# Weight low parts on VectorE alone, keys split straight into their own half, and a planner that may wait before it chooses

## The chip, the cores and the metric

The kernel runs on one core of a Trainium2 chip. The metric is device time in microseconds (us) of one execution. A core has five instruction streams that matter here: TensorE (PE in the profile, with its weight loads as PEld), VectorE (DVE), ScalarE (ACT), GpSimd (POOL) and SyncE (SP), which issues all of this kernel's DMAs.

## The reference

One layer of a hybrid decoder, 512 tokens of width 1024, all in float32. Cut to what matters:

```python
proj = rmsnorm(x, ln_mix_g) @ w_in                # 1024 -> 7728 columns
dq, dk = rope(rmsnorm(...)), rope(rmsnorm(...))   # 8 heads x 2 x 64
y_diff = (softmax(q0 k0) - lam * softmax(q1 k1)) @ v     # causal, 8 heads
k_cmp, v_cmp = gelu(blocks(k) @ w1) @ w2 ...      # compressed keys and values
y_nsa  = g0 * cmp + g1 * selected + g2 * window   # 16 heads, 4 key groups
mixed  = sig(m0) * (y_diff @ w_proj_diff) + sig(m1) * (y_nsa @ w_proj_nsa)
x = x + mixed @ w_out
x = x + square(relu(rmsnorm(x) @ w_mlp_up)) @ w_mlp_down
```

## The kernel before

**Two parts for a number.** A float32 operand of a matmul is held as a high part (a copy rounded to the type `F32R`) and a low part (operand minus high part), and a product is three matmuls: high by high, high by low, low by high. `split(hi, lo, src)` makes the parts: a copy that ACT or DVE does, then a subtraction on the engines in `lo_engs`.

**Weights.** `WStream` brings the weights as pieces of 128 x 1024 (`wraw`, two buffers) by a DMA of SP, and splits each in two halves of 512 columns into `whi` and `wlo` (two buffers each). `add`, in the last part of the kernel, hands every piece but those of the first chunk to the stream with `("DVE", "POOL")` as the engines that may subtract. The first chunk's four pieces are handed over near the start, also with both.

**The streams.** The PE order is first written by generators that a small driver (`Pe.run`) interleaves: a filler (all the large matmuls in a fixed plan: projections, merge gates, output projection, MLP) and four hot streams (rope, compressed keys, values, scores). The projections and the attention share the time up to about 660 us; after that only the output projection and the MLP are left.

**Keys.** `rope_stream` takes a finished projection chunk, normalises and rotates it (`norm_rope`, on ACT, DVE and POOL, with the power for the inverse square root on POOL), transposes a pair of key vectors into one PSUM bank (`ptp`, two banks) and calls `k_dups`. The two vectors of a pair lie in partitions 0 to 63 and 64 to 127. The scores need each vector in all 128 partitions (the query's high part meets it in one half, the low part in the other). `k_dups` splits the bank into one SBUF buffer `kp` (a single buffer), and four DMAs copy from there to the upper and the lower half of two key tiles `kk` (three buffers). There are 12 such pairs: 8 for the differential heads, 4 for the other branch.

**The planner.** `note` collects every instruction; `flush` then orders them by a list schedule with a price for each instruction (`price`), a latency between engines, and one shared resource, `port`: an instruction for which `ported` is true (a POOL instruction, or a DVE instruction of four kinds with all operands in SBUF, if its largest operand has 64 elements or more) isn't planned to run beside another such one. An instruction with more than one allowed engine goes to the one that takes it first. All instructions are then emitted from line 357, so every group of the profile has that line, and names of tiles tell them apart. The plan sets the order on each engine; on the chip each engine runs its list in order and waits for semaphores.

The lines that choose when the port is taken:

```python
if not put_off[-1][1].port[e]:
    p, op = put_off.pop()
else:
    p, op = put_off.pop(0)
...
op.start = max(t, self.port) if op.port[e] else t
```

Of the kernel before, what the change touches and what calls it, by code (L numbers as in the profile page):

```python
# [12 lines left out]
F32R = mybir.dt.float32r  # L13
AF = mybir.ActivationFunctionType
OP = mybir.AluOpType
# [116 lines left out]
class Sched:  # L132
# [34 lines left out]
    def price(self, eng, method, aps, k):  # L167
        if "accum_out" in k:
            aps = [x for x in aps if x is not k["accum_out"]]
        n = max(self.size(x) for x in aps)  # L170
        psum = any(self.tiles[x.tensor.name].space == "PSUM" for x in aps if x.tensor.name in self.tiles)
        if eng == "PE":
            if method == "transpose":
                return 113.0
            return max(113.0, 5.5 + self.size(aps[-1]) * 0.4315)
        if eng == "ACT":
            return (51 if psum else 93) + n * 0.8333 + (93 if "accum_out" in k else 0) + (
                93 if any(self.size(x) == 1 for x in aps[1:]) and n > 1 else 0)
        if eng == "DVE":
            ptr = sum(1 for x in aps[1:] if self.size(x) == 1) if n > 1 else 0  # L180
            if method in ("tensor_scalar", "tensor_copy") and not psum:
                return 69 + n * 0.52 + 61 * ptr
            if method == "memset":
                return 8 + n * 1.04
            if method == "reciprocal":
                return 69 + n * 6.25
            return 69 + n * 1.042 + 61 * ptr
        if eng == "POOL":
            if k.get("op") == OP.pow:
                return 300 + n * 165.0  # L190
            return 150 + n * 2.1
        return 20.0
# [2 lines left out]

    def ported(self, eng, method, aps, k):

        if max(self.size(x) for x in aps) < 64:
            return False
        if eng == "POOL":  # L200
            return k.get("op") != OP.pow
        return eng == "DVE" and method in self.TWICE and not any(
            self.tiles[x.tensor.name].space == "PSUM" for x in aps if x.tensor.name in self.tiles)

# [67 lines left out]
    def flush(self):  # L272

        ops, self.ops = self.ops, []
        self.wait = {e: [] for e in self.free}
        ok = {e: [] for e in self.free}
        fresh, again = [], set()
        for op in ops:
            for b in op.bufs:
                if b.group is None or b in again:  # L280
                    continue
                again.add(b)
                if b.granted:
                    self.held[b.group] += 1
                else:
                    fresh.append(b)
        for b in fresh:
            self.held.setdefault(b.group, 0)
            self.queue.setdefault(b.group, []).append(b)
        for op in ops:  # L290
            op.left, op.ready = 1, 0.0
            for d in op.deps:
                if d.left == -1:
                    op.ready = max(op.ready, d.end + self.lat(d.eng, op.eng, op.deps[d]))
                else:
                    d.users.append(op)
                    op.left += 1
            for b in op.bufs:
                if not b.granted:
                    b.waiting.append(op)  # L300
                    op.left += 1
        for g in list(self.queue):
            self.grant(g, 0.0)
        for op in ops:
            self.arm(op)
        done = []
        while len(done) < len(ops):
            best = None
            for e in self.free:
                for h, k in ((self.wait[e], 2), (ok[e], 1)):  # L310
                    while h and h[0][k].left == -1:
                        heapq.heappop(h)
                t = self.free[e] if ok[e] else max(self.free[e], self.wait[e][0][0]) if self.wait[e] else None
                if t is not None and (best is None or t < best[0]):
                    best = (t, e)
            assert best is not None, "no instruction can go on"
            t, e = best
            while self.wait[e] and self.wait[e][0][0] <= t:
                _, p, op = heapq.heappop(self.wait[e])
                if op.left == 0:  # L320
                    heapq.heappush(ok[e], (p, op))
            p, op = heapq.heappop(ok[e])
            if op.port[e] and self.port > t:
                put_off = [(p, op)]
                while ok[e] and put_off[-1][1].port[e]:
                    z = heapq.heappop(ok[e])
                    if z[1].left == 0:
                        put_off.append(z)
                if not put_off[-1][1].port[e]:
                    p, op = put_off.pop()  # L330
                else:
                    p, op = put_off.pop(0)
                for z in put_off:
                    heapq.heappush(ok[e], z)
            op.eng = e
            op.start = max(t, self.port) if op.port[e] else t
            op.end = op.start + op.ways[e][1]
            if op.port[e]:
                self.port = op.end
            self.free[e] = op.end  # L340
            if op.dma:
                self.hw = max(op.end, self.hw) + op.dma[0]
                self.dma = max(self.hw + 650, self.dma) + op.dma[1]
                op.end = self.dma
            op.left = -1
            done.append(op)
            for u in op.users:
                u.ready = max(u.ready, op.end + self.lat(e, u.eng, u.deps[op]))
                self.arm(u)
            for b in op.bufs:  # L350
                b.left -= 1
                b.end = max(b.end, op.end)
                if b.left == 0 and b.group is not None:
                    self.held[b.group] -= 1
                    self.grant(b.group, b.end + 150)
        for op in sorted(done, key=lambda o: o.start):
            op.ways[op.eng][0](*op.a, **op.k)  # L357
            op.ways = op.a = op.k = op.users = op.deps = None
# [68 lines left out]
def hybrid_block(ctx: ExitStack, tc: tile.TileContext, x, ln_mix_g, w_in, dqg, dkg, lq1, lk1, lq2, lk2,  # L427
# [4 lines left out]
    V, A, P, T, Q = (Engine(sched, n, e) for n, e in (("DVE", nc.vector), ("ACT", nc.scalar), ("POOL", nc.gpsimd),  # L432
                                                      ("PE", nc.tensor), ("SP", nc.sync)))
# [3 lines left out]
    def pool(stack, name, space="SBUF"):  # L437
        kw = {} if space == "SBUF" else {"space": getattr(MT, space)}
        return Pool(sched, stack.enter_context(tc.tile_pool(name=name, bufs=1, **kw)), space)
# [10 lines left out]
    def f(ap):  # L450
        return ap.bitcast(F32)
# [4 lines left out]
    def copy(out, src, engs=("ACT", "DVE")):  # L456
        sched.note([(e, COPY[e], getattr(sched.engs[e], COPY[e])) for e in engs], (out, src), {})

    def tt(out, a, b, op, engs=("DVE",)):
        sched.note([(e, "tensor_tensor", sched.engs[e].tensor_tensor) for e in engs], (out, a, b), {"op": op})  # L460

    def split(hi, lo, src, hi_engs=("ACT", "DVE"), lo_engs=("DVE",)):

        copy(hi, src, hi_engs)
        tt(lo, src, f(hi), OP.subtract, lo_engs)
# [11 lines left out]
    ws = WStream(wp, split)  # L477
# [87 lines left out]
    with ExitStack() as ps:  # L565
        pg = pool(ps, "pg", "PSUM")
        pscore = pool(ps, "pscore", "PSUM")
        ptr = pool(ps, "ptr", "PSUM")
        pav = pool(ps, "pav", "PSUM")

        att = pool(ps, "att")
# [316 lines left out]

        def k_dups(pt, key):

            kp = att.tile([128, 2, 512], F32R, tag="kp", bufs=1, name="kp")
            split(kp[:, 0, :], kp[:, 1, :], pt)
            if key[0] == "dk":
                kk = k_tile()
                dst = [kk[:, s] for s in range(2)]
            else:

                if key[2] == 0:
                    for s in range(2):
                        group_keys[key[1], s] = k_tile()  # L900
                dst = [group_keys[key[1], s][:, key[2]] for s in range(2)]
            for s in range(2):
                for d in range(2):
                    Q.dma_start(f(dst[s][d * 64:(d + 1) * 64]), f(kp[s * 64:(s + 1) * 64]))
            return dst

        jobs = []
# [633 lines left out]
        def add(gen, pieces):  # L1541
            for piece in pieces:
                load, width = piece if isinstance(piece, tuple) else (piece, 1024)
                ws.add(load, ("DVE", "POOL"), width)
            plan.append(gen)

        def eight(src):
# [101 lines left out]
```

## Time and profile before

| | before |
|---|---|
| time, median of 3 runs | 1096.38 us (1095.64 to 1096.85) |
| profiled execution | 1096.69 us, of which its span 1094.9 us |
| PE busy | 1053.8 us, 96% of the span |
| DVE busy | 766.2 us, 70% |
| POOL busy | 477.0 us, 44% |
| ACT busy | 465.6 us, 43% |
| mean granted TensorE clock | 0.990 |

The span is from the first to the last instruction of the profiled execution. Busy time counts instructions from start to end, including time in which one is held up inside; it isn't a rate. A row of a timeline gives the start, the duration, the engine, the operation, the tiles (out<-in) and, in brackets, the idle time of the engine just before, with what ended it.

### The profile page before, as it was taken

To read this page: it belongs to the slowest core of one execution; us is meant where nothing else is said; L and a number is where in the kernel's file an instruction comes from. 1 tells how busy PE (TensorE), PEld (TensorE's weight loads), DVE (VectorE), ACT (ScalarE), POOL (GpSimd) and SP (SyncE) were. 2 spreads that over 40 slices of the span, in tenths; PEclk is the share of its full clock that TensorE was granted. 3 is DMA by queue.
4 is the path that set the end of the run, shared out by engine and by line. 5 is a ranking of instruction groups with operands and counts; after the bars stand their busy time and mean duration, and the time that the engine had idled before them with its cause. 6 is when DMAs were issued, how large, how long until landed. Compare 5 with 4: busy or idle time off the path is not lost.

```text
span 1094.9 us, 15737 instructions
## 1 busy us (share of the span) xinstructions
PE 1053.8 (96%) x5257; PEld 875.6 (80%) x5257; DVE 766.2 (70%) x1905; ACT 465.6 (43%) x1136; POOL 477.0 (44%) x475
## 2 busy tenths in 40 slices
PE   6999988899999999999999998999999999999998
PEld 5877867788787888887788886788888888888886
DVE  6779678899988999999989898556533323354232
ACT  4257335656464466665456563214222111242110
POOL 3745698348767372292212024423333222333221
PEclk9999988999999999999999999999999999999999
DMA  6362534642654224536363255622322223332232
GB/s 209 97 173 63 153 102 120 163 132 71 172 143 142 64 78 137 142 125 214 129 193 112 92 161 170 208 85 94 96 97 97 97 96 96 97 97 96 97 136 75
DMA packets 83616, 134.66 MB, mean 123 GB/s; under 512 B 8784, under 2 KB 33872, under 8 KB 83536
## 3 DMA queue, kind: packets, MB, share of 16 engines
q1 hardware_dynamic: 83536, 133.67, 39.7%
q8 instruction: 41, 0.67, 0.3%
q14 instruction: 39, 0.32, 0.1%
HBM read 106.64 MB, written 14.42 MB: 111 GB/s over the span
## 4 chain that ended last, share of the span: by engine, by line
PE 74%; DVE 12%; DMA 6%; POOL 4%; issue 2%; SPq 1%; ACT 1%; DVEq 0%; POOLq 0%; ACTq 0%
PE gb L357 38%; PE ga L357 22%; PE sb L357 4%; PE avn L357 4%; PE ptn L357 3%; DMA kk<-kp 3%; DVE p L357 2%; POOL str L357 1%; PE av L357 1%; POOL wlo L357 1%; SPq L357 1%; POOL t1r L357 1%; DVE al L357 1%; DVE sm L357 1%; DMA kk<-in_x_dram 1%
## 5 line engine op out<-in xcount | busy, mean ns | idle before, releaser
L357 POOL TENSOR_TENSOR wlo<-wraw,whi 128x512 fp32r<-128x512 f32 x203 | 289.0, 1432 | 522.7 <-ACT whi L357 396.2
L357 ACT CAST whi<-wraw 128x512 fp32r<-128x512 f32 (+2 forms) x217 | 130.0, 618 | 343.7 <-PE gb L357 167.0
L357 DVE CAST whi<-wraw 128x512 fp32r<-128x512 f32 x97 | 47.5, 489 | 199.7 <-PE ga L357 95.8
L357 PE MATMUL gb<-wlo,hTh 128*128 128x512 f32 (+2 forms) x352 | 136.0, 388 | 4.4 <-POOL wlo L357 2.4
L357 PE MATMUL gb<-whi,hTl 128*128 128x512 f32 (+2 forms) x352 | 135.0, 384 | 0.0
L357 PE MATMUL gb<-whi,hTh 128*128 128x512 f32 (+2 forms) x352 | 133.4, 388 | 1.5 <-ACT hTh L357 1.3
L357 DVE CUSTOM_DVE_ANT_0 p<-sb,cst 128x512 f32<-128x512 f32 (+2 forms) x192 | 92.1, 481 | 13.1 <-PE sb L357 11.7
L357 DVE TENSOR_TENSOR wlo<-wraw,whi 128x512 fp32r<-128x512 f32 (+1 forms) x111 | 92.2, 832 | 7.2 <-ACT whi L357 2.7
L357 ACT ACTIVATE p<-p,smn 128x512 f32<-128x512 f32 (+3 forms) x128 | 72.0, 563 | 26.6 <-DVE smn L357 26.2
L357 PEld LDWEIGHTS gb<-wlo,hTh 128*128 128x128 f32 x352 | 67.7, 192 | 14.8 <-POOL wlo L357 3.4
L357 PEld LDWEIGHTS gb<-whi,hTh 128*128 128x128 f32 x352 | 66.7, 191 | 11.5 <-ACT hTh L357 1.7
L357 PEld LDWEIGHTS gb<-whi,hTl 128*128 128x128 f32 x352 | 67.6, 192 | 10.3 <-DVE hTl L357 0.3
L357 DVE TENSOR_SCALAR p<-p,smn,gates 128x512 f32<-128x512 f32 (+3 forms) x128 | 66.9, 527 | 1.0
L357 PE MATMUL gb<-big,whi 128*128 128x512 f32 x192 | 65.1, 403 | 0.0
L357 PE MATMUL gb<-hTl,whi 128*128 128x512 f32 x160 | 64.7, 404 | 0.0
L357 PE MATMUL gb<-hTh,wlo 128*128 128x512 f32 x160 | 64.5, 403 | 0.0
L357 PE MATMUL gb<-hTh,whi 128*128 128x512 f32 x160 | 64.0, 400 | 0.0
L357 DVE TENSOR_TENSOR al<-ptn,ah 128x128 fp32r<-128x128 f32 (+3 forms) x128 | 61.3, 482 | 3.6 <-ACT ah L357 2.0
L357 PE MATMUL ga<-h2l,whi 128*128 128x512 f32 x160 | 62.5, 391 | 0.0
L357 PE MATMUL ga<-h2h,whi 128*128 128x512 f32 x160 | 62.4, 391 | 0.0
L357 PE MATMUL ga<-h2h,wlo 128*128 128x512 f32 x160 | 62.3, 390 | 0.0
L357 ACT CAST ah<-ptn 128x384 fp32r<-128x384 f32 (+3 forms) x98 | 41.2, 424 | 49.1 <-PE ptn L357 38.1
(248 smaller groups left out, 2634.7 us busy)
## 6 DMA issues: line engine op xcount, KB each, us to landing
wraw<-in_w_in_dram SPq DMA_DIRECT2D x36, 512.0 KB, 3.6
wraw<-in_w_mlp_up_dram SPq DMA_DIRECT2D x32, 512.0 KB, 3.8
wraw<-in_w_mlp_down_dram SPq DMA_DIRECT2D x32, 512.0 KB, 3.5
kk<-kp SPq DMA_DIRECT2D x48, 256.0 KB, 4.5
wraw<-in_w_in_dram SPq DMA_DIRECT2D x36, 256.0 KB, 3.2
big<-yd SPq DMA_DIRECT2D x16, 512.0 KB, 3.4
yd<-yo SPq DMA_DIRECT2D x8, 512.0 KB, 3.3
wraw<-in_w_proj_diff_dram SPq DMA_DIRECT2D x8, 512.0 KB, 4.3
```

The source lines that it names most:

```text
L357: op.ways[op.eng][0](*op.a, **op.k)
```

## The change

Three edits. The weights handed over by `add` have their low parts made by DVE alone (those of the first chunk may still go to POOL). `k_dups` has no `kp` any more: for each of the two vectors of a pair it splits the vector's 64 partitions from PSUM straight into the same partitions of its key tile, and one DMA copies them to the other 64. The planner prices a `scalar_tensor_tensor` on one element per partition higher, counts small DVE instructions among those that need the port, and where all ready instructions of an engine need the port and it is taken, leaves the engine open until the port is free or another instruction becomes ready, and chooses then.

```diff
@@ price, DVE
-            ptr = sum(1 for x in aps[1:] if self.size(x) == 1) if n > 1 else 0
+            ptr = sum(1 for x in aps[1:] if self.size(x) == 1) if n > 1 else method == "scalar_tensor_tensor"
@@ ported
-        if max(self.size(x) for x in aps) < 64:
-            return False
         if eng == "POOL":
-            return k.get("op") != OP.pow
+            return k.get("op") != OP.pow and max(self.size(x) for x in aps) >= 64
         return eng == "DVE" and method in self.TWICE and not any(
@@ flush
-                if not put_off[-1][1].port[e]:
+                go = not put_off[-1][1].port[e]
+                if go:
                     p, op = put_off.pop()
-                else:
-                    p, op = put_off.pop(0)
                 for z in put_off:
                     heapq.heappush(ok[e], z)
+                if not go:
+                    self.free[e] = min(self.port, self.wait[e][0][0]) if self.wait[e] else self.port
+                    continue
             op.eng = e
-            op.start = max(t, self.port) if op.port[e] else t
+            op.start = t
@@ k_dups
-            kp = att.tile([128, 2, 512], F32R, tag="kp", bufs=1, name="kp")
-            split(kp[:, 0, :], kp[:, 1, :], pt)
...
             for s in range(2):
-                for d in range(2):
-                    Q.dma_start(f(dst[s][d * 64:(d + 1) * 64]), f(kp[s * 64:(s + 1) * 64]))
+                own, other = slice(s * 64, s * 64 + 64), slice(64 - s * 64, 128 - s * 64)
+                split(dst[s][own, 0], dst[s][own, 1], pt[own])
+                Q.dma_start(f(dst[s][other]), f(dst[s][own]))
             return dst
@@ add
-                ws.add(load, ("DVE", "POOL"), width)
+                ws.add(load, ("DVE",), width)
```

## Rows read from the trace of the kernel before

**Rows 1.** The page, busy time of each engine.
```profile
PE 1053.8 (96%) x5257; PEld 875.6 (80%) x5257; DVE 766.2 (70%) x1905; ACT 465.6 (43%) x1136; POOL 477.0 (44%) x475
```
**Rows 2.** Windows: stretch, length, busy us (instructions) of PE, PEld, DVE, ACT, POOL; clock, DMA.
```profile
136.90:219.00 82.10, 71.90 (x361) 58.89 (x359) 66.93 (x166) 41.73 (x107) 57.17 (x69) 0.90 0.48 128
...
410.60:656.90 246.30, 242.82 (x1335) 202.77 (x1334) 229.39 (x694) 149.18 (x396) 77.51 (x65) 1.00 0.46 145
```
**Rows 3.** The tile `kp`: minimum/median/maximum ns, waits of its instructions, and landing.
```profile
L357 DVE TENSOR_TENSOR kp<-ptp,kp x12: 629/684/692, 60.7 to 445.8; 128x512 fp32r<-128x512 f32 x12
...
  DMA kk<-kp: 11.4, 6
...
DMA to landing us min/median/max: 2.9/4.5/6.5
```
**Rows 4.** Timelines of DVE and PE around a refill of `kp`.
```profile
198.62 0.69 DVE L357 CAST kp<-ptp 128x512 fp32r<-128x512 f32 x1 [2.84 <-DMA kk<-kp]
...
199.84 0.50 PE L357 MATMUL sb<-kk,qa 128*128 128x256 f32 x2 [2.40 <-DVE sm L357]
```
**Rows 5.** Timeline of PE behind three other refills of `kp`.
```profile
71.83 0.50 PE L357 MATMUL sb<-kk,qb 128*128 128x512 f32 x1 [1.06 <-DVE sm L357]
...
291.24 0.70 PE L357 MATMUL sb<-kk,qb 128*128 128x512 f32 x2 [1.26 <-DVE sm L357]
...
321.45 0.39 PE L357 MATMUL av<-vt,al 128*128 128x256 f32 x1 [0.78 <-DVE al L357]
```
**Rows 6.** Timelines of DVE, POOL and PE, 170 to 176 us.
```profile
170.25 0.21 DVE L357 SCALAR_TENSOR_TENSOR sm<-sm,lam 128x1 f32<-128x1 f32 x1
...
173.77 1.22 DVE L357 SCALAR_TENSOR_TENSOR sm<-sm,lam 128x1 f32<-128x1 f32 x1
...
173.21 1.76 POOL L357 TENSOR_TENSOR wlo<-wraw,whi 128x512 fp32r<-128x512 f32 x1
...
175.65 0.80 PE L357 MATMUL gb<-wlo,hTh 128*128 128x512 f32 x1 [1.82 <-DVE wlo L357]
```
**Rows 7.** Waits of PE: total us, times, longest.
```profile
PE ptp L357 <- DVE kp L357: 2.8, 1, 2.8
PE gb L357 <- POOL wlo L357: 2.4, 2, 1.7
```
**Rows 8.** Timelines of DVE and PE, the start of the output projections.
```profile
672.58 2.36 DVE L357 TENSOR_TENSOR big<-yr,big 128x512 fp32r<-128x512 f32 x2
...
673.31 0.80 PE L357 MATMUL ga<-big,whi 128*128 128x512 f32 x1 [3.29 <-DVE big L357]
```
**Rows 9.** Windows of PE alone in four stretches: busy, clock, DMA.
```profile
157.90:164.70 6.80, 6.05 (x17) 0.50 0.86 198
174.90:181.70 6.80, 6.05 (x21) 0.50 0.43 144
202.30:205.60 3.30, 3.04 (x14) 0.50 0.98 223
673.30:676.70 3.40, 3.39 (x8) 0.50 1.01 375
```
**Rows 10.** Groups by form: count, busy us, mean ns, idle before and its releasers.
```profile
L357 DVE TENSOR_TENSOR wlo<-wraw,whi 128x512 fp32r<-128x512 f32 x110 | 91.7, 834 | 7.2 <-ACT whi L357 2.7 <-issue 0.4
...
L357 DVE TENSOR_TENSOR qa<-ptp,qa 64x512 fp32r<-64x512 f32 x16 | 10.9, 684 | 0.9 <-ACT qb L357 0.5
```
**Rows 11.** Windows, 410.6 to 656.9 us, of POOL `wlo`, DVE `wlo` and DVE `whi`.
```profile
410.60:656.90 246.30, 54.16 (x41) 1.00 0.46 145
410.60:656.90 246.30, 7.27 (x7) 1.00 0.46 145
410.60:656.90 246.30, 12.04 (x13) 1.00 0.46 145
```
**Rows 12.** Windows of two slices of the same stage; columns as in rows 2.
```profile
492.70:520.10 27.40, 25.24 (x148) 20.64 (x147) 26.73 (x62) 14.49 (x31) 7.51 (x6) 1.00 0.67 214
...
574.80:602.20 27.40, 27.40 (x152) 22.98 (x151) 26.05 (x81) 18.60 (x49) 7.76 (x6) 1.00 0.35 112
```

## The prediction

> **What bounds the kernel now.** I read four views, from the coarse to the fine. The page first: PE is busy for 1053.8 of 1094.9 us [rows 1], so all that any edit can win is the 41.1 us in which PE stands, plus what a low clock costs it. The windows by stage next, to see who is near its limit where PE stands. From 137 to 219 us PE is busy for 71.9 of 82.1 us, its granted clock is 0.90, and POOL is busy for 57.2; from 411 to 657 us PE is busy for 242.8 of 246.3 us, and DVE, at 229.4, has only 16.9 us left [rows 2]. Then the waits and the timeline of PE, for what each stop ends with. Two kinds of stop stand out. In one, DVE stands at a `kp` copy that waits for the DMAs of the key pair before, and PE stands a little later because the scores' banks or low parts that DVE should have served are late [rows 4, 5]. In the other, DVE isn't idle but is held inside a small instruction while POOL subtracts a weight half [rows 6], or PE waits for POOL's half itself [rows 7]. Last, the windows of the clock: in four stretches, 20.3 us together, the granted clock is 0.50, which is 1.2 GHz of 2.4 [rows 9], and three of the four begin at or just after a stop of PE named in rows 4, 6 and 8. A matmul there takes twice as long, so such a stretch costs up to half its length, 10.2 us in all.
>
> **The change part by part.** The sum is made against the profiled execution, 1096.7 us, which is 0.3 us over the median, a difference below anything said here.
>
> *Keys.* What goes is the wait for `kp`: 11.4 us of idle time in 6 waits [rows 3], paid by ACT and DVE with everything queued behind them. PE's share is 2.40 us behind the refill at 198.6 us [rows 4] and 1.06, 1.26 and 0.78 us behind three more [rows 5], 5.5 us together. The stretch of low clock that follows the first lasts 3.3 us [rows 9], which costs up to 1.7. The most the edit can give is thus 7.2 us. What comes in its place: two subtractions of 64 partitions instead of one of 128. They cost the same, since 684 ns is the mean at 64 x 512 [rows 10] and 684 the median at 128 x 512 [rows 3]. So each of 12 pairs costs DVE 0.68 us more, 8.2 us in all, and one more copy, on ACT or DVE, of some 0.7 us [rows 4]. The bank `ptp` stays taken for about 1.4 us longer, and behind it on PE stand the next transposes, which have waited 2.8 us for `kp` already [rows 7]. SP issues 24 DMAs instead of 48, so each of SP's loads queued behind a pair passes two issues fewer. The second vector's copy starts 1.4 us later than before, but only two transfers, not four, share the engines; a landing took 2.9 us at the least and 6.5 at the most [rows 3], so the keys are ready between 1.4 us later and 2.2 us earlier (6.5 - 2.9 - 1.4). I count that as nothing, because scores of other heads and the projections' matmuls cover it. I take 5 us of the 7.2, the rest being paid back to the longer hold of the bank.
>
> *POOL leaves the weights.* POOL loses all halves but the first chunk's, in the attention stage 41 that took 54.2 us, 1.32 each [rows 11]. DVE gains as many of 0.68 us, the time of a subtraction that nothing holds. What goes with them is the hold: a `scalar_tensor_tensor` on one column takes 0.21 us alone and 1.22 beside POOL's half, and PE then stands 1.82 us for the `wlo` queued behind it on DVE [rows 6]. DVE's own halves average 834 ns [rows 10], 150 over the unheld time. From rows: PE's stop of 1.82 [rows 6]; 2.4 us of PE waiting for POOL's halves [rows 7]; of the 3.29 us for `big` at 673 us, where two subtractions took 2.36 us instead of 1.36 [rows 8], about 1.5, since the next two halves are now DVE's own. That is 5.7 us. The low clock after the first of these lasts 6.8 us, half of it 3.4; that after `big` lasts 3.4, half of it 1.7 [rows 9], of which I count 0.9. Together 10.0 us at most; I take 6, because a new order will put other instructions beside POOL's remaining work, and the rotation's multiplications on POOL still hold DVE.
>
> The 2.8 us for `ptp` [rows 7] and the 6.8 us of low clock behind it, 3.4 at most [rows 9], come from the stage where POOL is at 70% [rows 2]; 6.2 together. Without its halves POOL's power and rotation come sooner, but the longer hold of `ptp` acts here. I take half, 3.1.
>
> A rule of the Trainium skill bears on this. The row first: beside POOL's half the small instruction took 1.22 us instead of 0.21 [rows 6]. "SBUF — State Buffer", section "SBUF: two separate sides", says that the port pair that DVE and GpSimd share is a lock taken for a whole instruction, with no sharing of bandwidth. The row agrees. By that rule every hold by a weight half goes, and the part would give all 10.0; by the row it gives what I take, as other POOL instructions stay.
>
> *DVE pays.* In the attention stage, 411 to 657 us, 41 halves come to DVE [rows 11], 41 x 0.68 = 27.9 us onto 229.4 of 246.3 [rows 2], which is 257.3: over the stage by 11.0. Against that: DVE's own 7 halves there took 7.3 us [rows 11] and would take 7 x 0.68 = 4.8 unheld, 2.5 less; and its 13 copies of weight halves, 12.0 us [rows 11], can go to ACT, which is busy for 149.2 of 246.3 us [rows 2]. That leaves 257.3 - 14.5 = 242.8 us, 98.6% of the stage, less what POOL's halves hold of other DVE instructions, for which I have no sum. How near is too near? In one slice of this stage DVE is busy 26.73 of 27.4 us, 97.6%, and PE loses 2.2 us; in another it is 26.05, 95%, and PE loses nothing [rows 12]. So the price lies between nothing (DVE stays at 95%) and 19 us (2.16 x 246.3/27.4 = 19.4, all at 97.6%). I take 4, nearer the first, as the copies that ACT or DVE may do fall to ACT when DVE is full. In the MLP I cost DVE's halves at nothing: each piece of weights feeds 24 matmuls, and DVE has its next two halves to make in that time; were that cover gone, each half would cost its 0.68 us.
>
> *The planner's edits.* No row prices an order. Their gain is bounded by PE's remaining stops, their loss by the same size; the higher price and the wider `port` bring the plan nearer to rows 6. I count nothing.
>
> Sum: 1096.7 - 5 - 6 - 3.1 + 4 = 1086.6. I predict 1086.5 us.
>
> **The rivals.** *DVE becomes the bound* (the other side). Place: 411 to 657 us. Mechanism: softmax, low parts and weight halves queue on DVE, so score banks come free late and PE stands. For it: 98.6% in the sum above and the slice at 97.6% [rows 12]. Against it: the holds still uncounted and ACT's room. It decides from about 97% of the stage on. Price: the 11.0 us by which the load exceeds the stage, with only the keys' 5 us won: 1096.7 + 11.0 - 5 = 1102.7.
> The skill speaks for this rival: "Perfetto Trace Analysis", section "Optimizing Scalar/DVE Operations", says that offloading a saturated DVE, even to GpSimd, may make sense, and the change does the reverse; the same section warns that the shared port may undo it. The stage's 93% on DVE [rows 2] bears out the first, rows 6 the second.
>
> *The stops only move.* A list schedule with other prices is a different order; the chip departs from it somewhere else, and as much is lost there. For it: the stops named above make 5.5 + 1.8 + 2.4 + 3.3 + 2.8 = 15.8 of PE's 41.1 us, and the rest has no one cause that the change removes. Against it: the `kp` waits have one cause, and it is gone. Time 1096.7, give or take 2.
>
> *Everything comes.* All three maxima, 7.2 + 10.0 + 6.2 = 23.4, and DVE pays nothing: 1073.3.
>
> **How the numbers follow.** The main forecast has 0.53 (its own range 1080 to 1093), everything 0.09, stops only move 0.14, DVE bound 0.24. Without a difference means within 0.2%, 2.2 us, about what a measurement of this kernel can tell. Faster is the main forecast and everything, 0.62; same 0.14; slower 0.24. The range from 1075 to 1102 leaves out most of the ninth of cases at the low end and the upper half of the DVE-bound case, about 2 in 10.
>
> **What the profile after would show.** No instruction waits for a copy out of `kp`, 24 transfers within `kk`, and the score stops behind key splits gone: keys right. POOL `wlo` down to a few halves of the first chunk, DVE `wlo` at a mean near 690 ns instead of 834, and fewer or shorter stretches at clock 0.50 between 150 and 210 us: holds right. PE busy in 411 to 657 us at 240 us or more in as short a stage, DVE at or below 97%: the price right. The prediction is wrong if PE's waits there are for `sm`, `smn`, `al` or `wlo` of DVE in tens, or if the transposes of `ptp` wait for `kk` splits more than 3 us in all.

## The result, and the profile after

The changed kernel takes 1085.7 us, the median of 4 runs (1083.84 to 1088.18), against 1096.49 for the kernel before beside it: a ratio of 0.9896, interval 0.9881 to 0.9912, so 1.0% faster: 10.8 us by the medians, 11.4 by the ratio, which the table below goes by. The forecast was 1086.5. The sum came out; three of its terms did not, as the experiments show.

The page of the kernel after, busy time of each engine:

```profile
PE 1050.5 (97%) x5257; PEld 870.8 (80%) x5257; DVE 814.7 (75%) x2131; ACT 471.0 (44%) x1153; POOL 174.0 (16%) x256
```

The span is 1082.2 us, so PE stands for 31.7 us instead of the 41.1 of [rows 1], and is busy 3.3 us less for the same number of matmuls. POOL is busy for 303 us less and DVE for only 48.5 more. The windows of the same stages, columns as in [rows 2]:

```profile
136.90:219.00 82.10, 75.15 (x401) 62.52 (x400) 76.89 (x216) 47.69 (x127) 35.13 (x50) 0.96 0.43 122
...
410.60:656.90 246.30, 241.57 (x1303) 198.63 (x1302) 231.77 (x706) 142.32 (x375) 22.36 (x23) 1.00 0.44 139
```

From 137 to 219 us PE is busy 3.3 us longer than in [rows 2], at a clock of 0.96 instead of 0.90. In the attention stage DVE is busy for 231.8 of 246.3 us, 94%, hardly more than the 229.4 before, although it now makes all the weight halves. The windows of PE alone in the stretches of low clock, columns as in [rows 9]; one at the very end of the span is left out:

```profile
167.90:171.30 3.40, 3.09 (x10) 0.50 0.00 0
195.20:198.60 3.40, 3.40 (x18) 0.50 0.04 3
```

There are two, 6.8 us together, where [rows 9] has four with 20.3. The mean clock of this execution, 0.997, is the highest of the kernel's four runs (0.994 to 0.997), so the others had more of it. The group of DVE's weight halves by form, which answers to [rows 10]:

```profile
L357 DVE TENSOR_TENSOR wlo<-wraw,whi 128x512 fp32r<-128x512 f32 x310 | 206.7, 690 | 4.4 <-ACT whi L357 0.4 <-PE gb L357 0.2
```

The mean is 690 ns, with 310 halves instead of 110 at 834. The group has grown by 115 us (from 91.7), and yet DVE is busy for 48.5 us more in all, so its other instructions take less time than before. The key tile `kk`, its splits (minimum/median/maximum ns) and waits, answers to [rows 3]:

```profile
L357 DVE TENSOR_TENSOR kk<-ptp,kk x24: 672/688/696, 57.6 to 426.9; 64x512 fp32r<-64x512 f32 x24
...
  DMA kk<-kk: 2.2, 4
```

and the page's row of the key transfers (how many, KB each, median us to landing):

```profile
kk<-kk SPq DMA_DIRECT2D x24, 256.0 KB, 3.0
```

There are 24 transfers instead of 48. The 11.4 us of [rows 3] were refills that waited for a buffer that was still being read. The 2.2 us left are score matmuls and their weight loads that wait for the keys to arrive; no split waits for a transfer any more. What is now first among PE's waits, after the start:

```profile
PE ga L357 <- DVE big L357: 2.2, 2, 1.3
PE sb L357 <- DVE smn L357: 2.1, 4, 0.8
PE pta L357 <- DVE kk L357: 2.0, 1, 2.0
PE sb L357 <- DVE sm L357: 2.0, 4, 0.7
PE gb L357 <- DVE wlo L357: 1.7, 3, 0.7
```

The largest single stop left behind the start is 2.0 us, and it is the price of the key edit: the timelines of DVE and PE show transposes that wait for a bank which the longer key split still holds.

```profile
191.86 0.69 DVE L357 TENSOR_TENSOR kk<-ptp,kk 64x512 fp32r<-64x512 f32 x1
...
192.70 0.41 PE L357 MATMUL pta<-cst,p 128*128 128x128 f32 x2 [2.03 <-DVE kk L357]
```

### The profile page after: what moved, and what is told of

Read it like the earlier page. It is cut to its first block, busy times and chain, and to the rows that moved or that the text cites. A ratio compares the mean times of both kernels' runs of the same rounds, so it can differ in the third digit from the quotient of the medians.

```text
span 1082.2 us, 15537 instructions
## 1 busy us (share of the span) xinstructions
PE 1050.5 (97%) x5257; PEld 870.8 (80%) x5257; DVE 814.7 (75%) x2131; ACT 471.0 (44%) x1153; POOL 174.0 (16%) x256
## 4 chain that ended last, share of the span: by engine, by line
PE 74%; DVE 17%; DMA 3%; POOL 2%; issue 2%; ACT 1%; SPq 1%; DVEq 0%; ACTq 0%
PE gb L357 39%; PE ga L357 21%; PE sb L357 4%; PE avn L357 3%; DVE p L357 3%; PE ptn L357 2%; DVE wlo L357 2%; DVE kk L357 1%; PE av L357 1%; PE hb L357 1%; POOL str L357 1%; DVE al L357 1%; DMA kk<-kk 1%; DVE t1r L357 1%; DVE big L357 1%
## 5 line engine op out<-in xcount | busy, mean ns | idle before, releaser
L357 ACT CAST whi<-wraw 128x512 fp32r<-128x512 f32 x215 | 129.2, 618 | 331.9 <-PE gb L357 183.2
L357 DVE TENSOR_TENSOR wlo<-wraw,whi 128x512 fp32r<-128x512 f32 x313 | 208.0, 688 | 4.4 <-ACT whi L357 0.4
L357 DVE CAST whi<-wraw 128x512 fp32r<-128x512 f32 x99 | 42.3, 427 | 183.2 <-PE ga L357 91.9
L357 PE MATMUL gb<-whi,hTh 128*128 128x512 f32 (+2 forms) x352 | 130.7, 383 | 1.8 <-ACT hTh L357 1.2
L357 PEld LDWEIGHTS gb<-whi,hTl 128*128 128x128 f32 x352 | 66.8, 190 | 10.3 <-DVE hTl L357 0.8
L357 POOL TENSOR_TENSOR t1r<-rw,ropec 128x256 f32<-128x256 f32 (+2 forms) x41 | 32.3, 789 | 177.1 <-ACT rw L357 169.6
L357 PE MATMUL ga<-whi,u 128*128 128x512 f32 x192 | 59.6, 389 | 0.0
```

## The experiments

The theory under test is the prediction's: the keys' single buffer and the holds by POOL's halves cost the time, and the planner's edits nothing. Rivals: only the order gained; or DVE becomes the bound. Times are saved (minus) or lost against the kernel before on the same chip, the ratio's distance from 1 times 1096.5 us. The last column is the time in which PE stands, the span less PE's busy time, of the one profiled execution of each kernel; the kernel before has 41.1.

| kernel | ratio, interval | us against before | PE stands, us |
|---|---|---|---|
| halves on DVE alone | 0.9965 (0.9952 to 0.9978) | -3.8 | 40.1 |
| keys alone | 0.9935 (0.9918 to 0.9952) | -7.1 | 41.6 |
| planner alone | 1.0087 (1.0064 to 1.0111) | +9.5 | 53.0 |
| halves and planner | 0.9953 (0.9936 to 0.9970) | -5.2 | 40.5 |
| keys and planner | 0.9906 (0.9886 to 0.9926) | -10.3 | 35.7 |
| halves and keys | 0.9937 (0.9922 to 0.9952) | -6.9 | 37.0 |
| all three | 0.9896 (0.9881 to 0.9912) | -11.4 | 31.7 |
| before, other order | 0.9992 (0.9981 to 1.0003) | -0.9 | 44.4 |
| all three, other order | 0.9884 (0.9869 to 0.9898) | -12.7 | 30.7 |

A mere reordering of the kernel before moves the last column by 3.3 us, so smaller differences in it say nothing. PE's stops fall most where the keys' and the planner's edits come together.

**One edit alone: weight halves.**

```diff
-                ws.add(load, ("DVE", "POOL"), width)
+                ws.add(load, ("DVE",), width)
```

> Only the weights' low parts move to VectorE; keys and planner as before. Theory of holds (GpSimd's halves hold VectorE inside its own instructions): most of the gain of 10.8 us comes with this edit alone, 1088 to 1091 us, and VectorE's low parts fall from a mean of 834 ns to under 720. Theory of the key buffer: the waits for kp stay, so at most 3 us are won, 1093 to 1097. Rival that VectorE becomes the bound: over 1098, with VectorE above 97% of 411 to 657 us.

Measured: 1093.78 us, 3.8 us won. Of the theory of holds, half came true. In the group by form the holds are mostly gone:

```profile
L357 DVE TENSOR_TENSOR wlo<-wraw,whi 128x512 fp32r<-128x512 f32 x307 | 211.4, 714 | 4.9 <-ACT whi L357 0.9 <-PE gb L357 0.2
```

The mean fell from 834 to 714 ns, and yet the time fell by a third of what it does with all edits. The waits for `kp` stayed, 8.4 us in 5. The windows of the stretch in which [rows 2] have the clock at 0.90, columns as there:

```profile
136.90:219.00 82.10, 73.70 (x404) 60.14 (x403) 74.15 (x202) 46.74 (x126) 45.19 (x63) 1.00 0.53 149
```

PE gets through 404 matmuls in it at the full clock, more than the 361 of before, so in this execution the low clock there is gone with this edit alone. In the whole execution PE stands for 1.0 us less and is busy for 3.5 us less (1050.3 us), so most of what this edit wins by itself is clock and not stops.

**One edit alone: keys.**

```diff
-            split(kp[:, 0, :], kp[:, 1, :], pt)
...
+                split(dst[s][own, 0], dst[s][own, 1], pt[own])
+                Q.dma_start(f(dst[s][other]), f(dst[s][own]))
```

> Only the keys go straight to their own half; GpSimd still makes weight halves, planner as before. Theory of the key buffer: 5 us are won (my term), 1091 to 1092 us, and no VectorE or ScalarE copy waits for a transfer out of a key buffer. Theory of holds: under 2 us, 1095 to 1097, because the stops of 1.8 and 3.3 us beside GpSimd's halves stay.

Measured: 1090.44 us, 7.1 us won, the most of any single edit, and nearly the ceiling of 7.2 that the prediction had added up from the stops behind `kp` and the low clock after one of them. The page says where it was won:

```profile
PE 1048.6 (96%) x5257; PEld 872.6 (80%) x5257; DVE 767.2 (70%) x1914; ACT 472.9 (43%) x1151; POOL 477.7 (44%) x475
```

The span is 1090.2 us, so PE stands for 41.6 us, as long as in the kernel before; it is busy for 5.2 us less. The granted clock is 0.50 in 10.2 us before the end (6.8 us from 158.6, 3.4 us from 517.0) instead of the 20.3 of [rows 9]. The waits for `kp` are gone, but other stops have come, the longest of 4.2 us at 158.06 us, of transposes that wait for a bank of `ptp`. So the size came out, but in this execution the gain isn't the shorter stops that the prediction had added up.

**One edit alone: the planner.**

```diff
-        if max(self.size(x) for x in aps) < 64:
-            return False
...
-            op.start = max(t, self.port) if op.port[e] else t
+            op.start = t
```

> Only the planner's three edits (price, port for small VectorE instructions, open choice). My sum counts them at nothing: 1094 to 1099 us. Rival that the order is what gains: the plan keeps small VectorE instructions out of GpSimd's way, so that 5 us or more are won, under 1091.5.

Measured: 1107.71 us, 9.5 us lost; neither theory had this. The waits of `kp` in its profile:

```profile
  DMA kk<-kp: 19.1, 5
```

and the timelines of ACT and PE behind the longest of them:

```profile
444.85 0.59 ACT L357 CAST kp<-ptp 128x512 fp32r<-128x512 f32 x1 [4.42 <-DMA kk<-kp]
...
446.21 1.12 PE L357 MATMUL ptc<-cst,pc 128*128 128x128 f32 x4 [3.63 <-DVE kp L357]
```

In the new order the refills of the single buffer wait for 19.1 us in 5 waits instead of 11.4 in 6, single ones of over 4 us, with PE standing 3.6 us behind one. That these waits are not the whole of the loss is shown by the run with halves and planner below.

**The kernel before in another order.**

```diff
-SLACK = 250
+SLACK = 260
```

> The kernel before with the planner's allowance between engines at 260 ns instead of 250: the same instructions in another order. It says how far any new order moves the time. If orders are alike: within 2 us of 1096.5. If the order is luck of some per cent (the stops only move): 4 us or more away, either side, and then single edits of under 4 us can't be told from a reordering.

Measured: 1096.94 us, 0.9 us won, the interval touching no change. This reordering moves the kernel by about a us, and the one of the changed kernel below by 1.3. Differences of 3 us and more between the edits are thus hardly luck of such an order; two reorderings are too few to say more, and the planner's edits, which change the rule of choice, move the time by up to 9.5 us.

**Two edits: halves and planner.** The first and the third diff above.

> VectorE alone for the low parts, and the planner's edits; keys through kp as before. Terms that add: the changed kernel's 1085.7 us plus what the keys are worth, 5 us, so 1090 to 1092. If the keys are worth nothing beside the rest: 1085 to 1088.

Measured: 1092.76 us. Without the keys' edit 6.2 us of the 11.4 are missing, and the waits are there again:

```profile
  DMA kk<-kp: 17.2, 6
```

The run also bears on the planner's edits alone, from which it differs by the halves only. It waits nearly as long for `kp` (17.2 us against 19.1) and is 14.7 us faster. So the waits for `kp` by themselves are not the 9.5 us that the planner's edits lost alone; POOL's halves had a part in that loss, and which way was not told apart.

**Two edits: keys and planner.** The second and the third diff.

> Keys straight to their own half, and the planner's edits; GpSimd still makes weight halves. Theory of holds: 5 us or more over the changed kernel, 1090 to 1094. Theory of the key buffer: within 3 us of the changed kernel, 1084 to 1089.

Measured: 1087.04 us, 10.3 us won, and 1.1 short of all three. POOL's halves are thus worth about 1 us once the other two edits are in, and the intervals overlap. This is the theory of the key buffer's number, not that of the holds. Its group of POOL's halves by form suggests why little is left to win:

```profile
L357 POOL TENSOR_TENSOR wlo<-wraw,whi 128x512 fp32r<-128x512 f32 x113 | 150.3, 1342 | 601.1 <-DVE whi L357 410.6 <-ACT whi L357 131.1 <-PE gb L357 25.2
```

With its three edits the planner gives POOL 113 halves instead of 201 of its own accord (102 in the run with the planner alone), and the mean of DVE's halves is down to 719 ns.

**Two edits: halves and keys.** The first and the second diff.

> The two edits of the work without the planner's: if the planner is worth nothing, 1084 to 1088 us as the changed kernel; if its choice of order is what gains, 1090 or more.

Measured: 1090.55 us, 6.9 us won, no more than the keys alone. The planner's edits are thus worth 4.5 us in this company. The windows from 219 to 410.6 us, first of this kernel:

```profile
219.00:410.60 191.60, 183.95 (x1027) 154.58 (x1026) 175.92 (x519) 111.53 (x304) 86.84 (x134) 0.99 0.33 94
```

then of all three:

```profile
219.00:410.60 191.60, 188.85 (x1073) 160.25 (x1072) 184.33 (x554) 113.05 (x315) 75.36 (x126) 1.00 0.36 102
```

In the same 191.6 us PE gets through 46 more matmuls, and DVE is busy for 8.4 us more, with the planner's edits. Counted from the start, all three is 19 matmuls behind at 219 us and 27 ahead at 410.6.

**The changed kernel in another order.** The diff of the other reordering, on the changed kernel.

> The changed kernel with the planner's allowance at 260 ns instead of 250: another order of the same instructions. If its gain is of the work and not luck of one order: 1083 to 1089 us. If it was luck of one order: 1090 or more.

Measured: 1084.69 us. The gain holds in another order, so it isn't luck of the one.

**More load for DVE.**

```diff
-                self.split(hi[:, c], lo[:, c], self.raw[k][:, c], lo_engs=self.todo[k][1])
+                self.split(hi[:, c], lo[:, c], self.raw[k][:, c], lo_engs=self.todo[k][1], hi_engs=("DVE",))
```

> The changed kernel with the weights' high parts on VectorE alone too: some 41 copies of 0.43 us more for VectorE in 411 to 657 us, on top of 231.8 of 246.3 us, which makes 249 us, more than the stage is long. If VectorE is at its limit there, as the rival of the prediction has it, TensorE stands: 1090 us or more. If there is still slack (other copies that VectorE or ScalarE may do move to ScalarE): within 3 us of the changed kernel's 1085.7.

Measured: 1103.94 us (ratio 1.0069, 1.0050 to 1.0088), 18.2 us over the changed kernel. The windows from 219 to 410.6 us and of the attention stage:

```profile
219.00:410.60 191.60, 183.43 (x1017) 150.78 (x1016) 185.23 (x564) 90.49 (x265) 83.44 (x123) 1.00 0.33 93
...
410.60:656.90 246.30, 237.26 (x1279) 194.06 (x1278) 238.98 (x751) 128.52 (x350) 24.02 (x24) 0.99 0.43 136
```

In the attention stage DVE is busy for 239.0 of 246.3 us, 97.0%, and PE for 4.3 us less than in the changed kernel. But more than half of the loss lies ahead of it: counted from the start, PE is 78 matmuls behind the changed kernel at 410.6 us and 102 at 656.9. From 219 to 410.6 us DVE is at 96.7%, where the changed kernel has it at 96.2% (184.33 us, in the window of all three above) and PE gets through 1073 matmuls instead of 1017. So more work on DVE does cost time, as the rival has it, but not at a load of the attention stage that could be named. Whether the full DVE costs it, or the low parts that wait behind the longer queue for their high parts, was not told apart.

**Less load for DVE.** The same line with `hi_engs=("ACT",)`.

> The changed kernel with the weights' high parts on ScalarE alone: VectorE gives up about a third of these copies. If VectorE's load still costs time, 1080 to 1084 us; if it does not, within 2 us of 1085.7, or up to 4 us slower because a copy takes 0.62 us on ScalarE instead of 0.43 and the low part waits for it.

Measured: 1083.08 us (ratio 0.9871, 0.9853 to 0.9888), the fastest of all, 2.7 us under the next experiment, which ran on the same chip and whose work is that of the changed kernel but for transfers. Their intervals overlap a little, so a gain of this version is likely and not certain.

**As many key transfers as before.**

```diff
                 Q.dma_start(f(dst[s][other]), f(dst[s][own]))
+                Q.dma_start(kspare[s], f(dst[s][own]))
```

The added transfer writes a DRAM tile that nobody reads.

> The changed kernel with a second transfer after each key vector (its own half to a spare place in DRAM), so that 48 key transfers of 256 KB are issued as before the change, but no copy waits for a buffer that they read. If the keys' gain is the wait for the single buffer: within 2 us of 1085.7. If it is the fewer transfers: 3 to 7 us slower.

Measured: 1085.77 us (ratio 0.9900, 0.9882 to 0.9919), as the changed kernel. With 48 transfers the time stays, so halving their number is worth nothing that can be measured here. (The added ones write to DRAM and not to SBUF.) That leaves the wait for the single buffer and what came with the new split. A kernel that keeps `kp` but with two buffers, which would have tried the wait by itself, was not run.

**POOL's work beside DVE again.**

```diff
                 self.split(hi[:, c], lo[:, c], self.raw[k][:, c], lo_engs=self.todo[k][1])
+                if self.spare is not None and self.todo[k][1] == ("DVE",):
+                    self.again(self.spare[:, 0], self.raw[k][:, c], hi[:, c])
```

`again` is the same subtraction on POOL into the buffer that `kp` had been; it ends before the output projections.

> The changed kernel in which GpSimd makes every weight half of the attention a second time, into a spare buffer that nobody reads: VectorE keeps the whole load, and GpSimd's work beside it is back. Theory of holds: VectorE's instructions are held again, some 70 us of busy time come back before 660 us, and 6 us or more are lost (1092 or more). If the holds cost TensorE little once the keys no longer wait: under 3 us lost, 1084 to 1089.

Measured: 1164.9 us (ratio 1.0625, 1.0604 to 1.0646), 79 us over the changed kernel. The page, and the group of DVE's halves by form:

```profile
PE 1074.7 (93%) x5257; PEld 877.7 (76%) x5257; DVE 892.0 (77%) x2157; ACT 484.7 (42%) x1170; POOL 358.7 (31%) x361
```

```profile
L357 DVE TENSOR_TENSOR wlo<-wraw,whi 128x512 fp32r<-128x512 f32 x310 | 227.6, 760 | 7.8 <-ACT whi L357 3.9
```

DVE is busy for 892.0 us instead of 814.7, so 77 us of busy time came back, about the 70 that the theory of holds had foretold; the time lost is as large, far more than the 6 us from which on that theory would count. Only 21 us of the 77 are in the weight halves (760 ns instead of 690). The others are in the rest of DVE's instructions: `rw<-t1r,str` of 128x512 takes 919 ns in the mean instead of 704, `ys<-yt,sm` of 128x128 581 instead of 340. POOL's copy also keeps each piece's buffers longer, and the planner keeps DVE's instructions apart from it; neither was taken out by itself, so the run fits the holds as the main cause of its loss and doesn't prove them. It is no measure of the holds of the kernel before, where DVE had 200 halves fewer to make.

## Why the prediction was right, and where it wasn't

**Keys, 5 us.** The size is right: 6.2 us as the last edit of three, 7.1 alone. The number of transfers is not the cause (the run with 48). The waits for the buffer are gone in every kernel with the edit, but how that becomes time is only in part as the prediction had it. It counted 5.5 us of PE's stops. Beside the other two edits PE does stand for 31.7 us instead of 40.5; with the keys alone it stands as long as before, and the 5.2 us less of busy time, with half the low clock, are the gain. The cost that was set against it, the bank `ptp` held longer, is there as PE's largest single stop behind the start, 2.0 us.

**POOL leaves the weights, 6 + 3.1 us, DVE pays 4.** The mechanism was seen, the size was not. The mean of DVE's halves fell to 690 ns as foretold and low clock fell from 20.3 to 6.8 us, but what the edit is worth hangs on its company: 3.8 us alone, nothing beside the keys without the planner, 14.7 beside the planner's edits without the keys, and 1.1 us as the last of three. The sum had 5.1 net. The term that was mis-sized is the 6 us for holds, and a part of it was misread. PE waited only for the first of the two subtractions of `big` [rows 8]: it goes on at 673.31 us, 0.73 us after that one began. The second is the one that was held, and beside it POOL worked on `tm`, not on a weight half. What a half did hold there came earlier, for instance in the two `kk<-tm,kk` at 669.70 us, which took 2.36 us together. With the halves on DVE alone the stops for `big` are no shorter (3.9 us in two, instead of 3.3) and a stretch of low clock behind them stays.

By the rule of the Trainium skill, "SBUF — State Buffer", section "SBUF: two separate sides", that the shared pair of ports is locked for a whole instruction, every hold by a weight half goes with the halves. The mean of 690 ns agrees. The time did not follow the holds: with the keys' and the planner's edits, 10.3 of the 11.4 us come with 113 halves left on POOL.

Whether the low clock goes with this part is less clear than one run makes it look. From 137 to 219 us the clock is 1.00 with the halves on DVE alone and with halves and keys, but 0.94 with halves and planner, and 0.96 with the keys alone and with all three, each in one execution. The 3.1 us can't be told from the rest of the 3.8 that the edit won alone.

**DVE pays.** The sum had DVE at 98.6% of the attention stage less holds without a number; it is 94.1%, near the slice that the prediction showed without loss, [rows 12]. PE is busy there for 1.3 us less than in [rows 2], a rough figure, since the windows of two kernels don't hold quite the same work; the sum took 4. That it decides from about 97% of DVE on is not borne out: the run with more load loses more than half of its time ahead of this stage, and from 219 to 410.6 us the changed kernel has DVE at 96.2% with PE busy for 98.6%. The Trainium skill, "Perfetto Trace Analysis", section "Optimizing Scalar/DVE Operations", says that offloading a saturated DVE, even to GpSimd, may make sense. Here the reverse, with DVE at 93% of the stage before, cost nothing that can be measured: as the last edit it won 1.1 us, with intervals that overlap.

**The planner's edits, nothing.** This step failed. Their worth goes from +9.5 us alone to -4.5 us as the last edit. Alone, the new order waits 19.1 us for `kp`, but the run with halves and planner waits 17.2 and is 14.7 us faster, so the loss needs POOL's halves too. As the last edit they give PE 46 more matmuls from 219 to 410.6 us. That terms may be added up was the tacit assumption; the edits interact. That the sum is right within 1 us is in part luck: POOL's part was too large by about what the planner's was too small. The keys' edit is worth between 3.1 us (beside the halves) and 19.8 (beside the planner's edits), always with the same sign.

**The rivals.** That the stops only move is out for the changed kernel, since another order of it is as fast; it fits the keys alone, where PE stands as long as before. Everything coming, 1073, did not: PE still stands for 31.7 us. DVE did not become the bound. Why the halves give nothing beside the keys without the planner's edits, although DVE is held less, is settled no further than that.

## What to carry to other kernels

Look at a single buffer between an engine and DMAs by what waits for it, not by how often it is filled: taking out 11.4 us of waits on ACT and DVE won 3 to 7 us of a kernel bound by TensorE, and 19.8 beside the planner's edits. Judge edits that share engines together, and in more than one company: the same edits of a planner lost 9.5 us alone and won 4.5 as the last of three. And read from PE's own stops whether an edit won what it was made for: the keys alone won 7.1 us without PE standing any less. A helper engine that takes work at half the speed may be doing little for the time: 303 us of POOL's busy time went, for 48.5 us more on DVE.

## What was not expected of the hardware

The subtraction of 128 x 512 on DVE averages 690 ns in the changed kernel and averaged 834 beside POOL's halves, but most were not held at all. Of the 110 in the trace of the kernel before, 23 took over 900 ns, and 21 of these began while a half of POOL ran; the other 87 took at most 705 ns, and 4 of them began so. When POOL made every half a second time, DVE's halves rose only to 760 ns, but DVE was busy for 77 us more in all and the kernel lost 79 us: the cost of the two engines side by side is read from DVE's whole busy time, hardly from its costliest group.

DVE's share of a stage doesn't say by itself whether DVE is the bound. At 96.2% from 219 to 410.6 us the changed kernel kept PE busy for 98.6% of the time; at 91.8% of the same stretch (175.92 us) the kernel with halves and keys kept it busy for 96.0%.
